# Another order for the first nine products of a fused matmul-tanh-multiply kernel, with new planned landing times, finer sums of the weights and later last multiplications

## The chip, the core and the metric

The kernel runs on one core of a Trainium2 chip. The metric is the time of one execution on the device, in microseconds (us). Before the change the median of three runs is 303.63 us, the lowest 303.56 and the highest 304.0.

The engines are named as in the profile: PE is the matrix engine (TensorE), DVE the vector engine, ACT the scalar engine, POOL the GpSimd engine, SP the engine that here only issues transfers. Each works through its own list of instructions in order. Transfers are issued by SP, ACT and POOL and then run on 16 DMA engines.

## The reference

```python
"x": np.random.randn(batch, m, k)     # 16 x 512 x 1024, float32
"w1": np.random.randn(k, n)           # 1024 x 768
"w2": np.random.randn(k, n)           # 1024 x 768

def reference(x, w1, w2):
    y1 = np.matmul(x, w1)
    y2 = np.matmul(x, w2)
    return (np.tanh(y1) * y2).astype(np.float32)
```

## The kernel before

The 8192 rows of x are 64 tiles of 128 rows. The inner dimension is 8 blocks of 128, in a lower and an upper half of 4 blocks. The columns of both weight matrices are three blocks of 512: `a` is w1[:, :512], `b` is w2[:, :512], and `g` holds the last 256 columns of w1 and of w2 side by side. Operands are cast to 16 bits, sums are float32.

**Head.** Tiles 0 to 3 are computed plainly (`plain`, `mm`, L426): per tile and column block eight matmuls, one for each inner block, while the weights arrive. One of these groups, `g` of tile 3, is left for the very end. `finals` then registers the tanh (ACT, L429) and the multiplication (DVE, L433) of a block; each frees the PSUM bank that the block occupied. There are eight banks.

**Triples.** The other 60 tiles are 20 triples of three tiles. A triple is three row tiles by two inner halves by three column blocks, which plainly would be 18 block products. The kernel does it with 15 products of sums (`C_OPS`, L24), `p0` to `p14`; each is four matmuls of 128x512 (`product`, L442). An operand is named by a mask of bits. For x, bits 1 and 2 are the lower and upper half of the triple's first tile, 4 and 8 those of the second, 16 and 32 those of the third. For w, bits 1, 2, 4 are the lower halves of blocks a, b, g and bits 8, 16, 32 their upper halves. Sums of x (`A_SUMS`; `x_sum`, L417, DVE, ten for each triple; below `S31` is the one with mask 31) are made from transposed x. Sums of w (`B_SUMS`; `w_sum`, L408, DVE, eleven in all; `B5` is the one with mask 5) are made once, in two halves of two inner blocks each.

Between the products the partial results are moved: copies and seeds on ACT (`c_copy`, L446), additions on DVE (`c_add`, L452), tanh on ACT (`c_tanh`, L455), multiplications on DVE (`c_mul`, L460). The ones that matter here: `add64` needs p7 and p10 and stands ahead of p12; `copy191` needs p12 and stands ahead of p11; `add312` needs p7 and p6 and stands ahead of p9; `seed56` needs p9 and stands ahead of both p8 and p14; `add4` comes after p3 and frees, at the end of a triple, a bank that p7 of the next but one triple takes. `abs_x` (L386, ACT) adds up the magnitudes of each x tile for a range test at the end.

**Data.** Tiles 4 to 63 of x are loaded with a cast by POOL (`load_x`, L358). From tile 7 on a transfer issued by SP transposes them (`transpose`, L383); a load waits, by a small cast on POOL (`hold_loads`, L479), until the transposition of the tile four before it has landed. Stores (L423) are on SP too, between the transpositions. The loads of `b` on POOL stand behind `gate` (L482), which waits for the first cast of `g`.

**Order.** Nothing is reordered while it runs. A planner (`Planner`, L74) puts every operation into its engine's list beforehand, with assumed costs and transfer times. The products have one fixed sequence, made of `FIRST_ORDER` (the nine products of triple 0 that start first), `PE_ORDER` (an entry with `+` runs within the following triple's fifteen) and `LAST_ORDER`. Each product has a nominal `slot_of` time, which counts from `START`. The due times of all other work are derived from these slots. A sum of x may in the plan not start before the slot of its first use less `S_AHEAD`:

```python
ORIGIN = START - 6 * SLOT
slot_of = {(i, p): ORIGIN + z * SLOT for z, i, p in sequence}
...
hold=needed(i, v) - S_AHEAD if i > 1 else 0.0,
```

When an engine is free the planner takes what can start first and, among those, what is due first (`pick`). `shared_landings` works out when the head's loads are assumed to land, from a size in us for each load and a latency for each queue. A product that begins in a new bank takes the bank that is free first; operations marked `seeds` need a bank that was last filled whole.

Every operation is one instruction, or four for a product, and each engine keeps the plan's order, so each instruction of the trace can be given its operation's name by counting along its engine. The names below are found so; `p7.10` is p7 of triple 10. Transpositions are named by tile: T36 is that of tile 36, the third tile of triple 10.

Of the kernel before, what the change touches and what calls it, by code (L numbers as in the profile page):

```python
# [66 lines left out]
)  # L67

PE_ORDER = "7 0+ 13+ 6 10 4+ 5+ 9 12 1 14 3+ 2+ 11 8"
FIRST_ORDER = "7 10 1 12 6 11 9 14 8"  # L70
LAST_ORDER = "0 13 4 5 3 2"


class Planner:  # L74
# [60 lines left out]
    def run(self):  # L135
        free = {"pe": 0.0, "act": 0.0, "dve": 0.0, "pool": 0.0, "sp": 0.0}
        bandwidth = 1.25
        left = {n: len(o["needs"] + o["behind"] + o["issued"]) for n, o in self.ops.items()}
        ready_at, end, engine_of, start_of = {n: o["hold"] for n, o in self.ops.items()}, {}, {}, {}
        ready = {e: [] for e in free}  # L140

        def release(n):
            for e in self.ops[n]["engines"]:
                ready[e].append(n)

        for n in self.ops:
            if not left[n]:
                release(n)
        position, lag = 0, 0.0
        strict = set(self.strict)  # L150
        while len(end) < len(self.ops):
            best = None
            for e, names in ready.items():
                options = []
                for n in names:
                    if n in strict and n != self.strict[position]:
                        continue
                    o = self.ops[n]
                    s = max(free[e], ready_at[n])
                    new = [c for c in o["chains"] if self.chains[c]["bank"] is None]  # L160
                    if new:
                        fit = self.fitting(o)
                        if not fit:
                            continue
                        s = max(s, min(fit)[0])
                    options.append((s, o["due"], n))
                if not options:
                    continue
                s, due, n = self.pick(e, options, lag)
                if best is None or s < best[0]:  # L170
                    best = s, e, n
            assert best, ("stuck", [(n, self.ops[n]["needs"]) for n in self.strict[position:position + 3]])
            s, e, n = best
            o = self.ops[n]
            for c in o["chains"]:
                if self.chains[c]["bank"] is None:
                    entry = min(self.fitting(o))
                    self.bank_free.remove(entry)
                    self.chains[c]["bank"] = entry[1]
                    if not o["seeds"]:  # L180
                        (self.partial.add if c[0] in ("T", "f") else self.partial.discard)(entry[1])
            f = s + o["engines"][e]
            free[e] = f
            if o["lands"]:
                done = o["lands"]
                bandwidth = max(bandwidth, done - 1.6)
            elif o["xfer"]:
                bandwidth = max(bandwidth, f) + o["xfer"]
                done = bandwidth + (o["latency"] or self.LATENCY["cast" if e == "pool" else "sp"])
            else:  # L190
                done = f
            end[n], engine_of[n], start_of[n] = done, e, s
            for k in o["engines"]:
                ready[k].remove(n)
            if n in strict:
                position += 1
                lag = s - o["due"]
            for c in o["chains"]:
                chain = self.chains[c]
                chain["end"] = max(chain["end"], done + self.LATENCY[e])  # L200
                chain["left"] -= 1
                if not chain["left"]:
                    self.bank_free.append((chain["end"], chain["bank"]))
            for u in self.next.get(n, ()):
                ready_at[u] = max(ready_at[u], f)
                left[u] -= 1
# [33 lines left out]
def kernel(  # L240
# [9 lines left out]
    B, M, K = x.shape  # L250
    _, N = w1.shape
    KO = K // P
    KH = KO // 2
# [3 lines left out]
    HEAD = 4  # L257
# [56 lines left out]
    op = plan.op  # L314
# [169 lines left out]
    MM = 0.2158  # L484
    SLOT = KH * MM
    CAST = {"a": {"dve": 0.37}, "g": {"act": 0.495}}
    START = 27.6
    ORIGIN = START - 6 * SLOT

    position = {}  # L490
# [5 lines left out]
    for n, p in enumerate(LAST_ORDER.split()):  # L496
# [7 lines left out]
    late = [f"b{k}" for s, k in slices if s == "b"]  # L504
    rows_in = (HEAD + 2, HEAD, HEAD + 1)
    GATE = ("g", 0)
    rings = [[(n, 0.75 + 0.3 * j, XW) for j, n in enumerate(on_sp)],
             [(f"a{k}", 0.75 + 0.45 * k, XW) for k in range(4)], [(n, 15.9 + 0.6 * j, 0.68) for j, n in enumerate(late)] + [(f"x{mt}", 22.0 + 0.6 * j, XX) for j, mt in enumerate(rows_in)]]
    lands = shared_landings(rings, 1.0, (2.1, 2.1, 2.6))

    for k in range(4):
# [66 lines left out]
    def finals(mt, s, due, last):  # L578
        if s != "b":
            lo, n = (0, F) if s == "a" else (F, G)  # L580
            op(f"th{s}{mt}", {"act": 0.5 if n == F else 0.28}, due, last, plain_tanh, mt, lo, n, (s, mt), 0,
               behind=reuse_out(mt), chains=[(s, mt)])
        if s != "a":
            lo, n, at = (0, F, 0) if s == "b" else (F, G, G)
            op(f"mu{s}{mt}", {"dve": 0.6 if n == F else 0.33}, due, last + [f"th{'a' if s == 'b' else s}{mt}"], plain_mul, mt, lo, n,
               (s, mt), at, chains=[(s, mt)])
            outs[mt].insert(0 if s == "b" else 1, f"mu{s}{mt}")

    for n, s in enumerate("agb"):
        for mt in range(HEAD):  # L590
            if (s, mt) == ("g", HEAD - 1):
                due, behind = (lambda n: 1e4 + n), [f"p0.{TRIPLES - 1}"]
            else:
                due, behind = (lambda n: landed[slices["agb".index(s) * KO + n]] + 0.8 + 0.02 * mt), []
            finals(mt, s, due(KO - 1) + (5.0, 3.0, 4.0)[n], plain(mt, s, due, behind))

    c_ops = {o[0]: o for o in C_OPS}
    readers = {}
# [10 lines left out]
            if u in a_readers:  # L609
                a_readers[u].append(f"S{v}")  # L610

    pieces = [slice(0, 2), slice(2, 4)]

    def w_needs(v, q):
        if v in wsum:
            return [f"B{v}.{q}"]
        bit = v.bit_length() - 1
        return [f"c{s}{k}" for s in "abg"[bit % 3] for k in range(bit // 3 * KH + pieces[q].start, bit // 3 * KH + pieces[q].stop)]

    for v, a, b, how in B_SUMS:  # L620
        for q, ks in enumerate(pieces):
            op(f"B{v}.{q}", {"dve": 0.6}, None, w_needs(a, q) + w_needs(b, q), w_sum, v, a, b, how, ks)

    def x_needs(i, v):
        if v & (v - 1):
# [13 lines left out]
    for i in range(TRIPLES):  # L639
# [10 lines left out]
        for o in C_OPS:  # L650
# [1 line left out]
            needs = [f"{n}.{i}" for n in needs]  # L652
            chains = sorted({(i, p) for p in o[3:6] if isinstance(p, str) and p[0] == "c"})
            if kind == "p":
                needs += x_needs(i, o[4]) + w_needs(o[5], 0) + w_needs(o[5], 1)
                op(f"{name}.{i}", {"pe": SLOT}, slot_of[i, name], needs, product, i, *o[3:], chains=chains)
                if not o[4] & (o[4] - 1):
                    xt_readers[HEAD + 3 * i + (o[4].bit_length() - 1) // 2].append(f"{name}.{i}")
                continue
# [35 lines left out]
    for mt in range(BY_PE, MT):  # L695
        back = xh_before(mt)
        free = [] if back is None else ([f"PT{back}0", f"PT{back}1"] if back < BY_PE else [f"T{back}"]) + ([f"D{back}"] if back >= HEAD else [])
        before = f"L{mt - 1}" if mt > BY_PE else f"L{rows_in[-1]}"
        if mt >= BY_PE + AHEAD:
            op(f"H{mt}", {"pool": 0.1}, None, [f"T{mt - AHEAD}"], hold_loads, mt - AHEAD, issued=[before])  # L700
            before = f"H{mt}"
        op(f"L{mt}", {"pool": 0.58}, None, [], load_x, mt, issued=[before], behind=free, xfer=XX)
        op(f"T{mt}", {"sp": 0.05}, None, [f"L{mt}"], transpose, mt, issued=[f"T{mt - 1}"] if mt > BY_PE else [],
           behind=xt_readers[mt - XT_BUFS] if mt >= XT_BUFS and mt - XT_BUFS != HEAD - 1 else [], xfer=1.2, latency=3.0)
    for mt in range(HEAD, MT):
        i, r = divmod(mt - HEAD, 3)
        soon = START + 1.1 * r if i == 0 else slot_of[i, "p7"] - 8 + 4.3 * r
# [125 lines left out]
```

## Time and profile before

| | us |
|---|---|
| median of three runs | 303.63 |
| profiled execution, its own time | 305.48 |
| span of the profiled execution, first to last instruction | 303.7 |
| PE busy | 291.2 |
| DVE busy | 254.0 |
| ACT busy | 224.5 |
| first product of the triples starts | 31.90 |
| last product's matmuls end | 298.12 |

The span is 1.78 us shorter than the profiled execution's own time and 0.07 us longer than the median of the runs without the profiler. A row of the timeline gives the start, the duration, the engine, the source line, what is written from what, how many instructions were merged and, in brackets, how long the engine stood idle before and what ended that. A matmul is shown with 0.38 us, but one follows the other every 0.216 us, so the idle time in the bracket is some 0.16 us less than the delay of the matmul's start. A row of the chain gives the start, the duration and what the time was spent on.

### The profile page before, as it was taken

The numbers are of one execution on the slowest core, as the hardware profiler recorded it, in microseconds if no ns is written. First come the engines' busy times: TensorE is split into PE (matmuls) and PEld (weight loads), VectorE is DVE, ScalarE is ACT, GpSimd is POOL, SyncE is SP. The second block draws the span as 40 slices with busy tenths as digits, with TensorE's granted clock in tenths as the row PEclk, the third lists the DMA queues.
The fourth block names the chain that finished last, engine by engine and source line by source line (L and its number), as shares of the span: only waits on it lengthen the run. The fifth ranks groups of instructions, "written<-read, shape, count | busy, mean of one in ns | idle before, by whom it ended". The sixth has DMA issues, their size and how long they took to land.

```text
span 303.7 us, 4640 instructions
## 1 busy us (share of the span) xinstructions
PE 291.2 (96%) x1377; PEld 133.3 (44%) x1377; DVE 254.0 (84%) x530; ACT 224.5 (74%) x451; POOL 49.6 (16%) x128
## 2 busy tenths in 40 slices
PE   8989989999999999999998999999999999999992
PEld 5435434444444444444443444444444444444440
DVE  1639999999797898978959898898989889898773
ACT  2687897688877988789787888767787767776542
POOL 0054032130301210212112111211121210000000
PEclk9999999999999999999999999999999999999999
DMA  7999999999999999999999999999999999131242
GB/s 232 385 290 208 169 124 144 175 203 236 187 158 222 190 276 281 154 205 277 210 225 241 238 245 230 249 254 190 254 280 164 299 246 253 77 155 52 104 190 92
DMA packets 84283, 63.51 MB, mean 209 GB/s; under 512 B 62752, under 2 KB 66336, under 8 KB 84256
## 3 DMA queue, kind: packets, MB, share of 16 engines
q1 hardware_dynamic: 73888, 45.36, 63.1%
q0 software_dynamic: 9792, 16.78, 38.2%
q10 hardware_dynamic: 576, 1.05, 1.0%
q8 instruction: 11, 0.18, 0.2%
q14 instruction: 16, 0.13, 0.2%
HBM read 39.85 MB, written 25.17 MB: 214 GB/s over the span
## 4 chain that ended last, share of the span: by engine, by line
PE 59%; DMA 26%; DVE 8%; ACT 2%; issue 2%; SPq 1%; ACTq 0%; POOL 0%; DVEq 0%; POOLq 0%
PE bank L442 55%; DMA xT<-xh 13%; DMA xh<-in_x_dram 7%; DMA arena<-in_w_dram 4%; PE bank L426 3%; DVE bank L452 3%; DVE o L460 2%; DVE early_x L417 2%; DMA wh<-in_w_dram 2%; ACT o L455 1%; ACT junk L386 1%; DVE arena L452 1%; PE bank L376 0%; ACTq L353 0%; DVE b L408 0%
## 5 line engine op out<-in xcount | busy, mean ns | idle before, releaser
L442 PE MATMUL bank<-b,early_x 128*128 128x512 f16 x640 | 148.4, 379 | 0.8 <-DVE arena L452 0.4
L442 PEld LDWEIGHTS <-early_x 128*128 128x128 f16 x800 | 78.1, 98 | 97.0 <-issue 3.4
L446 ACT ACTIVATE arena<-bank 128x512 f32<-128x512 f32 x100 | 58.7, 595 | 27.9 <-PE bank L442 27.8
L452 DVE TENSOR_TENSOR bank<-bank,arena 128x512 f32<-128x512 f32 x100 | 69.3, 694 | 10.5 <-ACT arena L446 4.2
L460 DVE TENSOR_TENSOR o<-o,bank 128x256 f32<-128x256 f32 (+1 forms) x120 | 63.1, 550 | 11.3 <-ACT o L455 9.9
L386 ACT ACTIVATE junk<-xh 128x1024 f16<-128x1024 f16 x60 | 63.3, 1055 | 0.3
L442 PEld LDWEIGHTS <-xT 128*128 128x128 f16 x400 | 38.9, 98 | 49.8 <-issue 4.0
L442 PE MATMUL bank<-b,xT 128*128 128x512 f16 x240 | 58.3, 379 | 0.0
L455 ACT ACTIVATE o<-bank 128x256 f32<-128x256 f32 x80 | 34.5, 437 | 18.2 <-DVE bank L452 15.8
L442 PE MATMUL bank<-wh,xT 128*128 128x512 f16 x160 | 40.9, 379 | 2.0 <-DVE bank L452 1.6
L442 PE MATMUL bank<-wh,early_x 128*128 128x512 f16 x160 | 41.0, 379 | 1.1 <-ACT bank L446 1.1
L358 POOL DMA_DIRECT2D xh<-in_x_dram x60 | 31.7, 528 | 35.4 <-PE bank L442 9.5
L479 POOL CAST held<-xT 128x1 f32<-128x1 f16 x53 | 12.8, 242 | 148.4 <-DMA xT<-xh 148.3
L417 DVE TENSOR_TENSOR early_x<-early_x,xT 128x512 f16<-128x512 f16 x80 | 31.8, 417 | 1.0 <-ACT xT L362 0.3
L446 ACT ACTIVATE bank<-bank 128x512 f32<-128x512 f32 x40 | 22.0, 579 | 11.0 <-PE bank L442 9.2
L455 ACT ACTIVATE o<-arena 128x512 f32<-128x512 f32 x40 | 25.1, 629 | 4.5 <-DVE arena L452 4.5
L426 PE MATMUL bank<-wh,xT 128*128 128x512 f16 x72 | 19.5, 379 | 1.5 <-DMA wh<-in_w_dram 0.9
L417 DVE TENSOR_TENSOR early_x<-xT,early_x 128x512 f16<-128x512 f16 x40 | 16.7, 417 | 5.0 <-DMA xT<-xh 5.0
L417 DVE TENSOR_TENSOR early_x<-xT,xT 128x512 f16<-128x512 f16 x40 | 16.7, 417 | 0.0
L452 DVE TENSOR_TENSOR bank<-arena,bank 128x512 f32<-128x512 f32 x20 | 13.8, 692 | 1.4 <-ACT o L455 1.3
L452 DVE TENSOR_TENSOR arena<-bank,arena 128x512 f32<-128x512 f32 x20 | 13.6, 679 | 0.0
L452 DVE TENSOR_TENSOR arena<-arena,bank 128x512 f32<-128x512 f32 x20 | 13.5, 677 | 0.0
(47 smaller groups left out, 133.8 us busy)
## 6 DMA issues: line engine op xcount, KB each, us to landing
out_dram<-o SPq DMA_DIRECT2D x60, 384.0 KB, 6.0
xh<-in_x_dram POOLq DMA_DIRECT2D x60, 256.0 KB, 7.1
arena<-in_w_dram SPq DMA_DIRECT2D x12, 256.0 KB, 5.5
early_x<-in_x_dram SPq DMA_DIRECT2D x8, 256.0 KB, 5.1
arena<-in_w_dram ACTq DMA_DIRECT2D x4, 256.0 KB, 5.9
wh<-in_w_dram POOLq DMA_DIRECT2D x8, 128.0 KB, 5.7
out_dram<-o SPq DMA_DIRECT2D x4, 256.0 KB, 2.5
xT<-xh SPq DMA_TRANSPOSE x57, 7.4
```

What stands on the lines that cost most here:

```text
L358: pin(nc.gpsimd.dma_start(xh(mt), xf[mt]))
L386: pin(nc.scalar.activation(junk[:, :src.shape[-1]], src, ACT.Abs, scale=scale, accum_out=sums[:, column:column + 1]))
L417: pin(engine[e].tensor_tensor(x_operand(i, v), x_operand(i, a), x_operand(i, b), OP[how]))
L426: pin(nc.tensor.matmul(bank(chain), xt(mt)[:, k, :], rhs, start=first, stop=k == KO - 1, skip_group_check=True))
L442: pin(nc.tensor.matmul(place(i, dst), x_operand(i, a)[:, k, :], w_rhs(b, k), start=begins and k == 0, stop=k == KH - 1, skip_group_check=T ...
L446: pin(nc.scalar.activation(place(i, dst), place(i, src), ACT.Copy, scale=float(sign)))
L452: pin(nc.vector.tensor_tensor(place(i, dst), a, b, ALU.add if signs == (1, 1) else ALU.subtract))
L455: pin(nc.scalar.activation(out_tile(HEAD + 3 * i + r)[:, lo:lo + n], place(i, src)[:, :n], ACT.Tanh, scale=float(sign)))
L460: pin(nc.vector.tensor_tensor(o, o, place(i, src)[:, at:at + n], ALU.mult))
L479: pin(nc.gpsimd.tensor_copy(held, xt(mt)[:, 0, :1]))
```

## The change

It has seven parts, all in what the planner is told:

1. `FIRST_ORDER` goes from `7 10 1 12 6 11 9 14 8` to `7 1 10 6 12 9 11 8 14`.
2. A product that opens a bank takes, among banks that are free in time, one that was last filled in part; before it was the one free first.
3. `START` goes from 27.6 to 28.6, and with it every slot, due time and hold of the triples.
4. The assumed sizes and start times of the head's loads are changed, which moves their assumed landings; the transposition of tiles 7, 8 and 9 gets an assumed latency of 1.0 in place of 3.0.
5. The last multiplication of a plain tile's `b` block is due 7.0 after the landing of the last weights, before 4.0.
6. The sums B5, B36, B37 and B45 (made of blocks a and g) are made in four quarters of one inner block, before in two halves.
7. A dictionary `FILL`, which is empty, changes nothing.

```diff
-FIRST_ORDER = "7 10 1 12 6 11 9 14 8"
+FIRST_ORDER = "7 1 10 6 12 9 11 8 14"
...
-                    entry = min(self.fitting(o))
+                    entry = min(self.fitting(o), key=lambda b: (b[0] > s, b[1] not in self.partial, b[0]))
...
-    START = 27.6
+    FILL = {}
+    FINE = (5, 36, 37, 45)
+    START = 28.6
...
-    rings = [[(n, 0.75 + 0.3 * j, XW) for j, n in enumerate(on_sp)],
-             [(f"a{k}", 0.75 + 0.45 * k, XW) for k in range(4)], [(n, 15.9 + 0.6 * j, 0.68) for j, n in enumerate(late)] + [(f"x{mt}", 22.0 + 0.6 * j, XX) for j, mt in enumerate(rows_in)]]
+    rings = [[(n, 0.75 + 0.3 * j, 0.75 if n[0] == "g" else 0.81 if n in ("x10", "x20", "x30") else XW) for j, n in enumerate(on_sp)],
+             [(f"a{k}", 0.75 + 0.45 * k, 0.81 if k else XW) for k in range(4)], [(n, 17.6 + 0.6 * j, 0.66) for j, n in enumerate(late)] + [(f"x{mt}", 22.0 + 0.6 * j, XX) for j, mt in enumerate(rows_in)]]
...
-            finals(mt, s, due(KO - 1) + (5.0, 3.0, 4.0)[n], plain(mt, s, due, behind))
+            finals(mt, s, due(KO - 1) + (5.0, 3.0, 7.0)["agb".index(s)], plain(mt, s, due, behind))
...
-    pieces = [slice(0, 2), slice(2, 4)]
+    PARTS = {v: 4 if v in FINE else 2 for v, *_ in B_SUMS}
+
+    def parts(v):
+        n = KH // PARTS[v]
+        return [slice(k, k + n) for k in range(0, KH, n)]
...
-        for q, ks in enumerate(pieces):
-            op(f"B{v}.{q}", {"dve": 0.6}, None, w_needs(a, q) + w_needs(b, q), w_sum, v, a, b, how, ks)
+        for ks in parts(v):
+            op(f"B{v}.{ks.start}", {"dve": {1: 0.335, 2: 0.6, 4: 1.13}[ks.stop - ks.start]}, None, w_needs(a, ks) + w_needs(b, ks), w_sum, v, a, b, how, ks)
...
-           behind=xt_readers[mt - XT_BUFS] if mt >= XT_BUFS and mt - XT_BUFS != HEAD - 1 else [], xfer=1.2, latency=3.0)
+           behind=xt_readers[mt - XT_BUFS] if mt >= XT_BUFS and mt - XT_BUFS != HEAD - 1 else [], xfer=1.2, latency=1.0 if mt < HEAD + 6 else 3.0)
```

More of the change, by code (lines that the diff above doesn't have):

```diff
@@ L593 @@
             else:
-                due, behind = (lambda n: landed[slices["agb".index(s) * KO + n]] + 0.8 + 0.02 * mt), []
-            finals(mt, s, due(KO - 1) + (5.0, 3.0, 4.0)[n], plain(mt, s, due, behind))
+                due, behind = (lambda n: landed[slices["agb".index(s) * KO + n]] + 0.8 + 0.02 * mt), [FILL[mt]] if s == "b" and mt in FILL else []
+            finals(mt, s, due(KO - 1) + (5.0, 3.0, 7.0)["agb".index(s)], plain(mt, s, due, behind))
     c_ops = {o[0]: o for o in C_OPS}
@@ L610, with w_needs @@
                 a_readers[u].append(f"S{v}")
-    pieces = [slice(0, 2), slice(2, 4)]
-    def w_needs(v, q):
+    PARTS = {v: 4 if v in FINE else 2 for v, *_ in B_SUMS}
+    def parts(v):
+        n = KH // PARTS[v]
+        return [slice(k, k + n) for k in range(0, KH, n)]
+    def w_needs(v, ks=slice(0, KH)):
         if v in wsum:
-            return [f"B{v}.{q}"]
+            return [f"B{v}.{p.start}" for p in parts(v) if p.start < ks.stop and ks.start < p.stop]
         bit = v.bit_length() - 1
-        return [f"c{s}{k}" for s in "abg"[bit % 3] for k in range(bit // 3 * KH + pieces[q].start, bit // 3 * KH + pieces[q].stop)]
+        return [f"c{s}{bit // 3 * KH + k}" for s in "abg"[bit % 3] for k in range(ks.start, ks.stop)]
     for v, a, b, how in B_SUMS:
-        for q, ks in enumerate(pieces):
-            op(f"B{v}.{q}", {"dve": 0.6}, None, w_needs(a, q) + w_needs(b, q), w_sum, v, a, b, how, ks)
+        for ks in parts(v):
+            op(f"B{v}.{ks.start}", {"dve": {1: 0.335, 2: 0.6, 4: 1.13}[ks.stop - ks.start]}, None, w_needs(a, ks) + w_needs(b, ks), w_sum, v, a, b, how, ks)
     def x_needs(i, v):
@@ L654 @@
             if kind == "p":
-                needs += x_needs(i, o[4]) + w_needs(o[5], 0) + w_needs(o[5], 1)
+                needs += x_needs(i, o[4]) + w_needs(o[5])
                 op(f"{name}.{i}", {"pe": SLOT}, slot_of[i, name], needs, product, i, *o[3:], chains=chains)
```

## The prediction

> **What bounds the kernel now.** I read the page first, then what PE waited for after 31 us, then PE's timeline, then the chain back from the largest wait, and last DVE's and ACT's timelines at those places. The page:
>
> ```profile
> span 303.7 us, 4640 instructions
> PE 291.2 (96%) x1377; PEld 133.3 (44%) x1377; DVE 254.0 (84%) x530; ACT 224.5 (74%) x451; POOL 49.6 (16%) x128
> DMA  7999999999999999999999999999999999131242
> PE 59%; DMA 26%; DVE 8%; ACT 2%; issue 2%; SPq 1%; ACTq 0%; POOL 0%; DVEq 0%; POOLq 0%
> ```
>
> PE is the bound by its length, but a quarter of the chain is transfers, and the DMA engines are busy in all slices to about 255 us. What PE waited for after 31 us:
>
> ```profile
> PE bank L442 <- DVE bank L452: 2.0, 3, 1.2
> PE bank L442 <- ACT bank L446: 1.1, 1, 1.1
> PE bank L442 <- DVE arena L452: 0.4, 1, 0.4
> PE bank L442 <- DVE o L460: 0.4, 1, 0.4
> ```
>
> These 3.9 us are all that a new order behind 31.9 us can win. PE's timeline shows where they lie:
>
> ```profile
> 22.36 0.81 PE L426 MATMUL bank<-wh,xT 128*128 128x512 f16 x3 [0.95 <-DMA wh<-in_w_dram]
> 31.90 1.89 PE L442 MATMUL bank<-wh,xT 128*128 128x512 f16 x8
> 33.63 1.03 PE L442 MATMUL bank<-b,early_x 128*128 128x512 f16 x4
> 35.06 3.83 PE L442 MATMUL bank<-b,early_x 128*128 128x512 f16 x16 [0.41 <-DVE arena L452]
> 39.99 1.02 PE L442 MATMUL bank<-wh,early_x 128*128 128x512 f16 x4 [1.09 <-ACT bank L446]
> 41.71 1.03 PE L442 MATMUL bank<-wh,xT 128*128 128x512 f16 x4
> 42.58 1.03 PE L442 MATMUL bank<-b,xT 128*128 128x512 f16 x4
> 55.29 1.02 PE L442 MATMUL bank<-wh,xT 128*128 128x512 f16 x4 [0.40 <-DVE o L460]
> 81.81 1.02 PE L442 MATMUL bank<-wh,xT 128*128 128x512 f16 x4 [0.46 <-DVE bank L452]
> 160.82 1.02 PE L442 MATMUL bank<-wh,xT 128*128 128x512 f16 x4 [1.16 <-DVE bank L452]
> 292.87 1.89 PE L442 MATMUL bank<-b,early_x 128*128 128x512 f16 x8 [0.34 <-DVE bank L452]
> ```
>
> An undisturbed product takes 0.865 us (from 41.71, p7.1, to 42.58, the next). The nine products of triple 0 run from 31.90 to 41.71: 9.81 us against 9 x 0.865 = 7.79, so 2.0 us are lost there. p12 starts at 35.06 where 33.63 + 0.865 = 34.50 would do: 0.57. Its group of 16 matmuls (p12, p6, p11, p9) and p14 behind it hold the other 1.45. The rows at 55.29, 81.81 and 160.82 are p7.2, p7.4 and p7.10; with 0.16 us added to each bracket they lose 0.56, 0.62 and 1.32. Without any of these waits p7.10 would start at 160.82 - 2.0 - 0.56 - 0.62 - 1.32 = 156.3.
>
> The chain back from the waits at 81.81 and 160.82, and what follows:
>
> ```profile
> 70.33 9.54 DMA xT<-xh
> 131.01 9.53 DMA xT<-xh
> 141.18 6.74 DMA xh<-in_x_dram
> 147.97 10.92 DMA xT<-xh
> 160.82 123.62 PE bank L442 x572
> ```
>
> The transposition T36 was issued at 147.97 and landed at 147.97 + 10.92 = 158.89; T18 at 79.87. Behind T36 stands the load of tile 36 (141.18), and behind that the landing of T32 (131.01 + 9.53 = 140.54): a loop of transfers that contains no product. From T32's landing to T36's are 18.35 us for four tiles, while PE needs 4/3 of 15 x 0.865 = 17.3. So in this stretch transfers set the pace. After 160.82 PE runs 123.6 us without a wait: a gain that stands at p7.10 reaches the end, and one that doesn't is lost.
>
> **The change part by part.** DVE's, ACT's and POOL's rows that carry the terms:
>
> ```profile
> 18.33 1.29 DVE L408 TENSOR_TENSOR b<-wh 128x1024 f16<-128x1024 f16 x2 [3.27 <-ACT wh L362]
> 22.84 1.29 DVE L408 TENSOR_TENSOR b<-wh 128x1024 f16<-128x1024 f16 x2 [1.76 <-ACT wh L362]
> 33.73 0.68 DVE L433 TENSOR_TENSOR o<-o,bank 128x512 f32<-128x512 f32 x1
> 34.33 0.68 DVE L452 TENSOR_TENSOR arena<-arena,bank 128x512 f32<-128x512 f32 x1
> 37.73 0.41 DVE L417 TENSOR_TENSOR early_x<-early_x 128x512 f16<-128x512 f16 x1
> 38.06 0.41 DVE L417 TENSOR_TENSOR early_x<-xT 128x512 f16<-128x512 f16 x1
> 51.62 0.41 DVE L417 TENSOR_TENSOR early_x<-xT 128x512 f16<-128x512 f16 x1
> 158.98 0.42 DVE L417 TENSOR_TENSOR early_x<-xT,early_x 128x512 f16<-128x512 f16 x1 [2.24 <-DMA xT<-xh]
> 159.32 0.74 DVE L460 TENSOR_TENSOR o<-o,bank 128x256 f32<-128x256 f32 x2
> 159.99 0.69 DVE L452 TENSOR_TENSOR bank<-arena,bank 128x512 f32<-128x512 f32 x1
> 22.17 1.16 ACT L362 CAST wh<-arena 128x512 f16<-128x512 f32 x2
> 38.30 1.06 ACT L386 ACTIVATE junk<-xh 128x1024 f16<-128x1024 f16 x1
> 39.27 0.19 ACT L386 ACTIVATION_READ_ACCUMULATOR junk<-xh 128x1 f32 x1
> 39.36 0.58 ACT L446 ACTIVATE bank<-bank 128x512 f32<-128x512 f32 x1
> 50.99 0.41 POOL L479 CAST held<-xT 128x1 f32<-128x1 f16 x1 [9.86 <-DMA xT<-xh]
> ```
>
> *Planned landings (part 4): nothing before 31.90.* No transfer is issued elsewhere. The wait at 22.36 is for the first `b` weights, and what could run ahead of it, the last `g` products, needs the casts that end only at 22.17 + 1.16 = 23.33. From 22.36 PE works through 38 plain matmuls and three tiles of transposes without a gap, in whatever order. Ends: -0.95 (that wait gone) to +0.87 (one group of four matmuls put ahead of its load). I take 0.
>
> *Order of the nine (part 1): -1.2 us of PE, between -2.0 and 0.* Every dependent pair now has one whole product between: p10, p6, p12 for `add64`; p6, p12, p9 for `add312`; p12, p9, p11 for `copy191`; p9, p11, p8 for `seed56`, where before p14 stood right behind p9. That gap is 0.865 - 0.16 = 0.70 us. An addition takes 0.69, so it fits with 0 to 0.1 left over; a seed takes 0.58. What can spoil it is ACT: at 38.30 a magnitude sum of 1.06 + 0.19 kept `seed56` waiting until 39.36, and such a sum may again stand ahead of it. At worst 1.25 of it is in the way, against a slack of 0.1; I take 0.75, for a sum begun a little earlier. The lower end of nothing is two such sums.
>
> *Late multiplications (part 5): included above.* The one at 33.73 is what delayed `add64` to 34.33, so p12 to 35.06. Moved back, it and its three fellows hold four banks for longer. Part 2 hands the first products the partly filled banks; p7's bank is free for `add312`. The first that needs one of the four is `seed56`; if its multiplication came late, that would cost one, 0.68. These 2.7 us of DVE work then stand among the sums for p0 and p13. The cover there is the quarters' gain, next.
>
> *Quarters (part 6): 0 on the path.* DVE idles 3.27 + 1.76 = 5.0 us around 18 to 23, waiting for casts of `g`. Four sums in quarters take 16 instructions every 0.33 us (37.73 to 38.06, the same shape) or 5.3, against eight at some 0.6 (two in 1.29, the ends overlapping), 4.8: 0.5 more, inside that idle time. Since a quarter waits for one cast pair, all four sums are done soon after 23.3; before, two of their halves ran later, in DVE's busy stretch. That takes 1.2 us out of it, less 0 to 0.5. The Trainium skill (Perfetto Trace Analysis, Optimizing Scalar/DVE Operations) says that each DVE operation on SBUF carries about 60 ns of its own, so larger ones are better on a saturated engine, but that breaking up can help where DVE isn't saturated and holds others up. By its figure eight more instructions are an estimated 0.5 us, and the trace agrees with that; DVE is idle there, so the second half of the rule applies.
>
> *START and the holds (part 3): decides where the gain ends.* On DVE S31.10 (158.98) waited 2.24 us for T36, and behind it in line stood two multiplications and `add4.8` (159.99), ready long before, for whose bank p7.10 waited. S31's hold is its slot less 4. Slots move 1.0 later. The planned start of the products also moves later, by about the 1.6 us that the first `b` load's assumed landing moves (1.7 for its start, little for the sizes), but the planned waits among the nine go, which as the trace has them are 2.0. So the holds fall about 1 us (0.2 to 1.4) behind the same products, and `add4`, 1.0 us behind S31 here, is likely to go first. Then only T36 itself holds p7.10: 158.89 + 0.05 = 158.94, where it was 160.82: -1.88. The same holds at p7.4: T18 at 79.87 for 81.81.
>
> *Transposition latency, slots against transfers: +0.3 on DVE, covered.* T10 landed just before 50.99 and S3.2 ran at 51.62. With PE and DVE 1.2 us earlier S3.2 waits for it, some 0.5 us, with everything behind it: p7.2, 3.7 us after S3.2 here, comes no earlier than 50.95 + 3.67 = 54.6 (-0.7). From there eight triples of 12.97 give 158.4, still below 158.94.
>
> The sum: 303.70 - 1.88 = 301.8 for the span; it stands 0.07 above the median, so 301.75 for the runs. The early gains of 0.7 to 4.5 us are worth 1.88 because T36 cuts them off, and 0.5 us of new early waits change nothing.
>
> **The rivals.** A change within 0.2% (0.6 us) is about what a measurement of this kernel can't tell from none.
>
> 1. *S31.10 stays ahead of `add4.8`.* Then DVE waits for T36 as before, and p7.10 starts at 160.8: 303.6. Against it: a hold moved by 0.1 us is enough if the multiplications behind are ready. Chance 0.14.
> 2. *Transfers come earlier too.* The loop is started by tile 10's load, which waits for a magnitude sum on ACT; transposition and store places on SP shift as well. p7.10 can go to 156.3 + 0.75 = 157.0, which is 299.8; half of it, 300.8. Against it: T36's chain has no product in it. Chance 0.2.
> 3. *Slower: one more store, or a late sum on ACT, puts the transfer loop back.* The loop's place is 36 to 159 us, its price 18.35/4 = 4.6 us for a tile's turn. Once T36 lands after 161.4 (2.5 us later, half a turn) the kernel is slower by over 0.6; a whole turn gives 158.94 + 4.6, 2.7 us over before: 306.3. For it: DMA busy at 9 tenths throughout, and stores that are ready earlier compete with the same transfers. The Trainium skill (DMA: Bandwidth & Descriptors, Issuing engines are not separate DMA queues) says that transfers from all issuing engines run on the same 16 DMA engines and interleave; the slices agree, and by that rule a faster PE wins no transfer time. Chance 0.18.
>
> **How the numbers follow.** My forecast, p7.10 held by T36 alone, has 0.48; T36 varies with neighbours by some 0.7 us, so its own range is 301.1 to 302.5. Faster: 0.48 + 0.2 = 0.68; same 0.14; slower 0.18. The range runs from 300.2, where a third of rival 2 is left out, to 304.4, where most of rival 3 is.
>
> **What would show it.** PE's timeline: p7.0 still at 31.9; the nine take 8.2 to 8.8 us; no wait over 0.8 among them. DVE: quarters of the sums between 17 and 24.5, no 128x1024 sum of `a` and `g` behind. p7.10 at 158.9 with its bracket naming the transfer, not DVE, and S31.10 behind `add4.8`. After that no wait to 284. Wrong would be: T36 away from 158.9 by over 1.5 us, p7.10 still waiting for DVE, or a new wait after 160 us.

## The result, and the profile after

Six runs of the changed kernel have a median of 301.83 us (301.65 to 302.66), six of the kernel before 303.7 (303.46 to 304.0). The ratio is 0.9943, with a 95% interval of 0.9931 to 0.9956: some 1.9 us less by the medians. A ratio compares only runs within 1.5% of the fastest run of their kernel; a median is over all runs. The forecast was 301.75. The number came out; the mechanism did not, as follows.

The page of the kernel after:

```profile
span 300.4 us, 4674 instructions
PE 290.8 (97%) x1377; PEld 132.8 (44%) x1377; DVE 255.8 (85%) x538; ACT 224.9 (75%) x451; POOL 52.5 (17%) x128
DMA  6999999999999999999999999999999999231243
PE 84%; DMA 7%; DVE 5%; issue 1%; ACT 1%; ACTq 0%; SPq 0%; POOL 0%; DVEq 0%
```

The profiled execution took 302.25 us by its own time. Transfers are 7% of the chain, where they were 26%. What PE waited for after 31 us is down from 3.9 us to 1.2:

```profile
PE bank L442 <- DVE o L460: 0.5, 1, 0.5
PE bank L442 <- DVE arena L452: 0.4, 1, 0.4
PE bank L442 <- DVE bank L452: 0.3, 1, 0.3
```

PE's timeline of after, at the places the prediction named:

```profile
32.09 1.03 PE L442 MATMUL bank<-wh,xT 128*128 128x512 f16 x4
36.09 3.70 PE L442 MATMUL bank<-b,early_x 128*128 128x512 f16 x16 [0.39 <-DVE arena L452]
40.75 1.04 PE L442 MATMUL bank<-wh,xT 128*128 128x512 f16 x4
54.42 1.02 PE L442 MATMUL bank<-wh,xT 128*128 128x512 f16 x4 [0.50 <-DVE o L460]
80.31 1.03 PE L442 MATMUL bank<-wh,xT 128*128 128x512 f16 x4
158.01 1.03 PE L442 MATMUL bank<-wh,xT 128*128 128x512 f16 x4
281.00 0.17 PE L473 MATMUL bank<-count,ones 128*128 128x8 bf16 x1
290.38 1.89 PE L442 MATMUL bank<-b,early_x 128*128 128x512 f16 x8 [0.34 <-DVE bank L452]
```

The nine products run from 32.09 to 40.75, 8.66 us (before: 9.81). p7.4 (80.31) and p7.10 (158.01) have no bracket: the two waits on which the forecast stood are gone, but the hold by T36, which the forecast put in their place, is not there either. The next rows are from POOL's timeline of after. They are the small casts that wait for T10 and for T36:

```profile
42.81 0.18 POOL L479 CAST held<-xT 128x1 f32<-128x1 f16 x1 [1.01 <-DMA xT<-xh]
144.05 0.20 POOL L479 CAST held<-xT 128x1 f32<-128x1 f16 x1
```

T10 had landed by 42.8 (before: 50.9). The cast behind T36 runs at 144.05 and did not wait for it; by the transfer's own record T36 landed at 141.85, 17 us earlier than the 158.89 that the forecast took for fixed.

The last DVE instructions and the last four stores of after, from the timeline of its end:

```profile
295.08 2.59 SPq L423 DMA_DIRECT2D out_dram<-o  x4
295.82 1.34 DVE L460 TENSOR_TENSOR o<-o,bank 128x256 f32<-128x256 f32 x3
```

The last multiplication ends at 295.82 + 1.34 = 297.16, and 3.2 us later the span is over. In the kernel before the same row stood as follows, and from its end at 299.65 to 303.7 it took 4.05 us:

```profile
298.31 1.34 DVE L460 TENSOR_TENSOR o<-o,bank 128x256 f32<-128x256 f32 x3
```

So the gain has a term at the very end that the prediction did not have.

### The profile page after: what moved, and what is told of

The parts are those of the page before. It is cut to its first block, busy times and chain, and to the rows that moved or that the text cites. A ratio compares the mean times of both kernels' runs of the same rounds, so it can differ in the third digit from the quotient of the medians.

```text
span 300.4 us, 4674 instructions
## 1 busy us (share of the span) xinstructions
PE 290.8 (97%) x1377; PEld 132.8 (44%) x1377; DVE 255.8 (85%) x538; ACT 224.9 (75%) x451; POOL 52.5 (17%) x128
## 3 DMA queue, kind: packets, MB, share of 16 engines
q10 hardware_dynamic: 576, 1.05, 1.0%
## 4 chain that ended last, share of the span: by engine, by line
PE 84%; DMA 7%; DVE 5%; issue 1%; ACT 1%; ACTq 0%; SPq 0%; POOL 0%; DVEq 0%
PE bank L442 80%; DMA arena<-in_w_dram 4%; PE bank L426 3%; DMA wh<-in_w_dram 2%; DMA xT<-xh 1%; DVE bank L452 1%; DVE o L460 1%; DVE early_x L417 1%; DVE arena L452 1%; ACT o L455 1%; PE bank L376 0%; ACTq L353 0%; DVE b L408 0%; ACT wh L362 0%; SPq L350 0%
## 5 line engine op out<-in xcount | busy, mean ns | idle before, releaser
L452 DVE TENSOR_TENSOR bank<-bank,arena 128x512 f32<-128x512 f32 x100 | 69.5, 695 | 19.1 <-ACT arena L446 13.2
L460 DVE TENSOR_TENSOR o<-o,bank 128x512 f32<-128x512 f32 (+1 forms) x120 | 61.1, 549 | 4.9 <-ACT o L455 3.2
L455 ACT ACTIVATE o<-bank 128x256 f32<-128x256 f32 x80 | 33.0, 436 | 12.4 <-DVE bank L452 8.2
L479 POOL CAST held<-xT 128x1 f32<-128x1 f16 x53 | 15.6, 295 | 39.5 <-DMA xT<-xh 39.4
```

The source lines that it names most:

```text
L452: pin(nc.vector.tensor_tensor(place(i, dst), a, b, ALU.add if signs == (1, 1) else ALU.subtract))
L455: pin(nc.scalar.activation(out_tile(HEAD + 3 * i + r)[:, lo:lo + n], place(i, src)[:, :n], ACT.Tanh, scale=float(sign)))
L460: pin(nc.vector.tensor_tensor(o, o, place(i, src)[:, at:at + n], ALU.mult))
L479: pin(nc.gpsimd.tensor_copy(held, xt(mt)[:, 0, :1]))
```

## The experiments

After the comparison three theories stood. The first is the forecast's: in the kernel before, T36 and what stands behind it on DVE hold p7.10 in every execution, and the new plan takes away DVE's part of that. The second: the new landings let the planner put the magnitude sum of tile 4 early, tile 10's load with it, and all transfers run ahead from there. The third: the profiled execution of before was not a typical one, and the gain comes from other places. All kernels compute the whole result.

**The kernel before once more** (no edit).

> The kernel before once more, for a second profiled execution. The first one took 305.48 us, 1.85 above the median of the plain runs, and lost 0.62 + 1.32 us at p7.4 and p7.10 to late transpositions. Theory A (the prediction's: T36 lands at 158.9 and caps everything): p7.10 again starts at 160 to 161, T36 lands at 158 to 159.5. Theory C (those two waits belong to that one execution): T36 lands at 157 or earlier, p7.10 loses under 0.3 us, the span is 301.5 to 302.5. Time 303.6 under either.

Measured: 303.94 us, ratio 0.998 (0.9946 to 1.0014); span of its profile 302.2. PE's timeline, POOL's cast behind T36, and ACT's magnitude sum of tile 4:

```profile
31.86 1.89 PE L442 MATMUL bank<-wh,xT 128*128 128x512 f16 x8
41.67 1.03 PE L442 MATMUL bank<-wh,xT 128*128 128x512 f16 x4
55.24 1.02 PE L442 MATMUL bank<-wh,xT 128*128 128x512 f16 x4 [0.40 <-DVE o L460]
81.24 1.02 PE L442 MATMUL bank<-wh,xT 128*128 128x512 f16 x4
158.94 1.02 PE L442 MATMUL bank<-wh,xT 128*128 128x512 f16 x4
```
```profile
148.58 0.18 POOL L479 CAST held<-xT 128x1 f32<-128x1 f16 x1 [2.88 <-DMA xT<-xh]
```
```profile
34.69 1.06 ACT L386 ACTIVATE junk<-xh 128x1024 f16<-128x1024 f16 x1
```

The same program, and T36 lands at 148.5 in place of 158.9; p7.4 and p7.10 wait for nothing. The waits among the nine and at p7.2 are the same as in the first profile. The forecast's theory falls: the two waits, 0.62 + 1.32 = 1.94 us, come in some executions and not in others. That execution took 305.48 us, 1.85 above the median of the plain runs; this one took 303.98, close to its median. Two more profiled executions further down, of kernels close to before, have one such wait each (0.69 at p7.4 in 305.39 us, 1.37 at p7.10 in 305.26 us). So this profile is the one to compare with:

| stretch | before, second profile | after | difference |
|---|---|---|---|
| start to p7.0 | 31.86 | 32.09 | +0.23 |
| p7.0 to p7.1, nine products | 9.81 | 8.66 | -1.15 |
| p7.1 to p7.2 | 13.57 | 13.67 | +0.10 |
| p7.2 to the last multiplication's end | 242.53 | 242.74 | +0.21 |
| from there to the span's end | 4.4 | 3.2 | -1.2 |
| span | 302.2 | 300.4 | -1.8 |

The +0.21 is the matmul of the range test: by the starts of the products around it, it costs 0.32 us in after (at 281.00) and 0.11 here. A third of the gain (0.6) lies ahead of the last multiplication's end, two thirds behind it. The rows of this execution's end:

```profile
295.69 3.61 SPq L423 DMA_DIRECT2D out_dram<-o  x4
296.43 1.34 DVE L460 TENSOR_TENSOR o<-o,bank 128x256 f32<-128x256 f32 x3
```

The four stores take 3.61 us to issue, against 2.59 in after; by its own record the last of them takes 1.40 us here and 0.38 there. The view of the DMA queues for the last 6.2 us of this kernel shows what else ran there (queue, kind, packets, MB, share; then the stores with KB each and us to landing):

```profile
q14 instruction: 3, 0.02, 1.8%
q8 instruction: 1, 0.02, 1.6%
...
out_dram<-o SPq DMA_DIRECT2D x3, 128.0 KB, 3.2
```

And for the last 4.9 us of after:

```profile
q14 instruction: 1, 0.01, 0.5%
...
out_dram<-o SPq DMA_DIRECT2D x2, 128.0 KB, 1.8
```

Transfers that fetch instructions run among the last stores. In the kernel before, one of queue 8 and three of queue 14 fall there, and a store lands after 3.2 us; in after one of queue 14, and a store lands after 1.8. Two runs further down test this.

**The new order alone, in the kernel before.**

```diff
-FIRST_ORDER = "7 10 1 12 6 11 9 14 8"
+FIRST_ORDER = "7 1 10 6 12 9 11 8 14"
```

> Before with the new order of the first nine products alone. Theory A: the nine take about 8.7 us in place of 9.8, but T36 stays at 158.9 and S31.10 stays ahead of add4.8, so the time stays at 303.4 to 303.7. Theory B (the gain needs the transfers to run ahead, which the magnitude sum of tile 4 decides, and its place does not change here): the same, 303.4 to 303.7, with T10 landing near 50. Theory C (the medians gained only what the nine products gained): 302.4 to 302.8.

Measured: 304.09 us, ratio 1.0006 (0.9977 to 1.0036). DVE, then PE:

```profile
33.79 1.88 DVE L433 TENSOR_TENSOR o<-o,bank 128x512 f32<-128x512 f32 x3
...
36.26 0.68 DVE L452 TENSOR_TENSOR arena<-arena,bank 128x512 f32<-128x512 f32 x1
```
```profile
36.99 3.88 PE L442 MATMUL bank<-b,early_x 128*128 128x512 f16 x16 [1.42 <-DVE arena L452]
```

Three multiplications of plain tiles stand ahead of `add64` (36.26), and p12 loses 1.58 us. The nine take 9.62 us, and the order by itself is worth nothing. T10 landed at 43.63 here, not near 50 as the expectation had it, and T36 at 144.94, though the magnitude sum of tile 4 had not moved; the transfers ran ahead and the time did not fall.

**The change without the later due time.**

```diff
-            finals(mt, s, due(KO - 1) + (5.0, 3.0, 7.0)["agb".index(s)], ...
+            finals(mt, s, due(KO - 1) + (5.0, 3.0, 4.0)["agb".index(s)], ...
```

> The changed kernel with the plain tiles' last multiplications due 4.0 after the weights, as before. With the new order alone, put into before, add64 stood behind three such multiplications and p12 lost 1.58 us. Theory: here too they go ahead of add64, p12 loses 1.2 to 1.8, the nine take 9.5 to 10 us and the time is 302.6 to 303.4. If the late due time is idle: 301.8.

Measured: 303.62 us, ratio 0.9969 (0.9946 to 0.9991). DVE, then PE:

```profile
34.98 1.88 DVE L433 TENSOR_TENSOR o<-o,bank 128x512 f32<-128x512 f32 x3
36.77 0.68 DVE L452 TENSOR_TENSOR arena<-arena,bank 128x512 f32<-128x512 f32 x1
```
```profile
37.50 3.78 PE L442 MATMUL bank<-b,early_x 128*128 128x512 f16 x16 [1.82 <-DVE arena L452]
```

The same picture from the other side: p12 loses 1.98 us and the nine take 9.91. Without the late multiplications the order does not pay. p7.2 starts 0.51 later than in after (54.93), and the end takes 4.38 us.

**The magnitude sum of tile 4 put back, in the changed kernel.**

```diff
-        op(f"D{mt}", ..., mt, hold=soon)
+        op(f"D{mt}", ..., mt, hold=soon + (4.0 if mt == HEAD else 0.0))
```

> The changed kernel with one thing more: the magnitude sum of tile 4 (D4) may not start before 4.0 us later in the plan, so on ACT it goes back behind the copy of p7, as before the change. In the changed kernel it ran at 30.2 us and the load of tile 10 was issued at 31.6 in place of 36.2. Theory B (D4's place puts all transfers ahead): T10 lands near 50 again, T36 near 158, the time is 302.8 to 303.5. Theory C: the transfers may come later but the time stays within 0.5 of the changed kernel's, 301.8 to 302.3. Theory A: T36 at 158.9 and a time of 301.7 to 302, as it had been forecast.

Measured: 303.79 us, ratio 0.9986 (0.9957 to 1.0016). POOL's cast behind T10, and PE at p7.2:

```profile
51.18 0.37 POOL L479 CAST held<-xT 128x1 f32<-128x1 f16 x1 [8.89 <-DMA xT<-xh]
```
```profile
55.09 1.02 PE L442 MATMUL bank<-wh,xT 128*128 128x512 f16 x4 [0.96 <-DVE o L460]
```

T10 lands at 51.06 again, x sums stand behind it on DVE, and p7.2 loses 0.67 of its gain. T36 lands at 154.98, p7.4 and others wait too, and no gain can be told from this ratio. So it matters that the new plan starts this sum at 30.18 and not at 34.7:

```profile
30.18 1.07 ACT L386 ACTIVATE junk<-xh 128x1024 f16<-128x1024 f16 x1
```

**That sum put early, in the kernel before.**

```diff
-        op(f"D{mt}", {"act": 1.05}, soon + 4, ...
+        op(f"D{mt}", {"act": 1.05}, -10.0 if mt == HEAD else soon + 4, ...
```

> Before with one thing changed: the magnitude sum of tile 4 is due first, so it goes ahead of the evacuations of tiles 4 and 5 on ACT, some 5 us earlier. Nothing else is told to the planner. Theory B: the load of tile 10 is issued by 32, T10 lands by 45, T36 by 145, the waits at p7.4 and p7.10 go and the time falls by 1 to 2 us, to 301.7 to 302.7; the nine products still take 9.8 us or some tenths more. Theory C: the transfers go ahead but the time stays at 303.4 to 304. Theory A: T36 moves little, 303.6.

Measured: 305.07 us, from 302.99 to 321.53 with five of twelve runs above 309, ratio 0.9986 (0.9964 to 1.0007). POOL's casts behind T10 and T36:

```profile
42.07 1.06 POOL L479 CAST held<-xT 128x1 f32<-128x1 f16 x1
...
158.48 0.44 POOL L479 CAST held<-xT 128x1 f32<-128x1 f16 x1 [4.29 <-DMA xT<-xh]
```

T10 lands early, at 41.76, and T36 late all the same, at 158.36, and p7.10 loses 1.37 us to it. The nine take 9.11 us, 0.7 less than in before, yet p7.2 starts at 55.33, no earlier. The second theory falls as a sufficient cause: an early start of the loop doesn't keep the transfers ahead. The early sum is needed in the new plan and brings nothing in the old one.

**More matmuls ahead of everything, in the kernel before.** The warm-up, which writes nothing that is used, gets 40 short matmuls in place of 14 long ones.

```diff
-    WARM = 14
+    WARM = 40
...
-    pin(nc.tensor.matmul(banks[...][:, :2 * P], ..., ones.bitcast(bf16), ...
+    pin(nc.tensor.matmul(banks[...][:, :88], ..., ones.bitcast(bf16)[:, :88], ...
```

> Before with 26 matmuls more in PE's list and as many columns as before in all: the 14 warming matmuls of 256 columns at the start become 40 of 88 columns (they compute nothing that is used). So PE's instructions stand 52 places later in its list. In three profiles of before's end an instruction fetch of 16 KB on queue 8 began 0.3 to 0.4 us before the last multiplication ended, and the end followed 4.1 to 4.45 us after that multiplication; in the changed kernel the fetch came 5.9 us before it, and the end 3.2 after. Theory D (the fetch slows the last stores, and its place follows the count of PE's instructions): the fetch moves some 5.5 us ahead, the end follows 3.1 to 3.4 us after the last multiplication, and the time falls by 0.8 to 1.2 us, to 302.5 to 302.9. Rival (the end differs for another reason): 4.1 to 4.5 us, time 303.5 to 304.

Measured: 304.07 us, ratio 0.9994 (0.997 to 1.0018). The fetch of queue 8 moved from 0.3 us to 13.2 us ahead of the last multiplication's end, further than the 5.5 expected. In the second profile of before, 218 to 305 PE instructions lie between one fetch of this queue and the next, so the queue very likely serves PE. In this profile the longer warm-up also put p7.0 at 32.73, 0.87 us later. But the end still took 4.37 us, and the view of its DMA queues has three fetches of queue 14 left there:

```profile
q14 instruction: 3, 0.02, 1.5%
...
out_dram<-o SPq DMA_DIRECT2D x2, 128.0 KB, 2.4
```

PE's fetch alone is not it.

**Idle instructions on three engines, in the kernel before.**

```diff
-    WARM = 14
+    WARM = 20
...
+    for n in range(20):
+        pin(nc.vector.memset(idle[:, :1], 0.0))
...
+    for n in range(8):
+        pin(nc.scalar.copy(idle[:, 1:2], ones[:, :1]))
```

> Before with small idle instructions added at the start, where each engine stands idle: 20 one-column fills on DVE, 8 one-column copies on ACT, and the warming matmuls as 20 of 176 columns in place of 14 of 256. The planned order stays. Moving PE's fetch alone did not shorten the end, since fetches on queue 14 remained 0.5 and 1.3 to 1.9 us after the last multiplication. Theory D, extended (any engine's instruction fetch among the last stores costs time, and its place follows the count of that engine's instructions): the fetches on queues 8 and 14 leave the stretch from 0.4 before to 1.9 us after the last multiplication, the end follows 3.1 to 3.5 us after it, before 4.05 to 4.45, and the time falls by 0.7 to 1.2. Rival: the end stays at 4.0 to 4.5 whatever the fetches do; 303.6 to 304.2.

Measured: 303.22 us, ratio 0.9974 (0.995 to 0.9998); beside it the kernel before had 304.15. PE's times stay as before (p7.1 at 41.59, p7.2 at 55.17). The end, and its DMA queues:

```profile
295.52 2.59 SPq L424 DMA_DIRECT2D out_dram<-o  x4
...
296.26 1.34 DVE L461 TENSOR_TENSOR o<-o,bank 128x256 f32<-128x256 f32 x3
```
```profile
q14 instruction: 1, 0.01, 0.6%
...
out_dram<-o SPq DMA_DIRECT2D x2, 128.0 KB, 1.8
```

From 297.60 to the span's end at 300.8 are 3.2 us, as in after. The last multiplication ends 0.17 us earlier than in the second profile of before, so all but that of the shorter span is the end. Work that does nothing makes the old kernel 0.9 us faster by the medians (0.1 to 1.5 by the interval), and in the profile the fetches have left the last stores. That is the term of -1.2 us, shown by itself.

**The change without quarters.**

```diff
-    FINE = (5, 36, 37, 45)
+    FINE = ()
```

> The changed kernel with the four w sums in halves again. Theory: the first quarter runs beside POOL's gate cast, which took 0.43 us in place of 0.18, so the b loads started 0.2 later; in halves the gate takes 0.18, the first b weights land near 22.3 and p7.0 starts at 31.85 in place of 32.09. Against that two halves return to DVE's busy stretch behind 24 us and p7.2 comes 0.3 to 1.2 later than that gains. Time 301.9 to 302.7. If the quarters do nothing: 301.6, by the gate alone.

Measured: 302.86 us, ratio 0.9953 (0.9926 to 0.9981). The nine take 8.04 us, less than with quarters, but p7.2 starts at 54.44, as in after. POOL's gate ahead of the `b` loads takes 0.18 us here and 0.44 in after, where it runs beside DVE's quarters; `b` still lands at 22.46 and p7.0 starts at 32.05. So the long gate is not why p7.0 is 0.2 late in after. The end takes 4.39 us, with queue 8's fetch in it. The quarters alone do not decide that: the change without the later due time has them, and its end takes 4.38 us with the same fetch. In this profile the quarters pay nothing ahead of p7.2; whether the better end is theirs is not shown.

**The change with the old order.**

```diff
-FIRST_ORDER = "7 1 10 6 12 9 11 8 14"
+FIRST_ORDER = "7 10 1 12 6 11 9 14 8"
```

> The changed kernel with the old order of the first nine products. Theory (the prediction's first term): p14 behind p9 waits for its seed again, the nine take 9.5 to 10 us in place of 8.66, p7.2 starts 0.7 to 1.3 later than 54.42, and the time is 302.5 to 303.2. Rival: what the nine give is taken by DVE's backlog before p7.2 in any case; then p7.2 stays within 0.3 of 54.4, and the time at 301.8 to 302.

Measured: 303.27 us, ratio 0.9974 (0.9956 to 0.9993). PE's timeline:

```profile
54.19 1.02 PE L442 MATMUL bank<-wh,xT 128*128 128x512 f16 x4
```

The nine take 9.06 us, 0.4 more, and p7.2 starts at 54.19, no later than in after. What the order wins among the nine, DVE's backlog ahead of p7.2 takes back; in these profiles the other parts do the early gain without it. From p7.0 to p7.2 the profiles have, in us:

| kernel | p7.0 to p7.2 |
|---|---|
| before, both profiles | 23.39, 23.38 |
| before with the new order | 23.52 |
| before with the early sum | 23.48 |
| after | 22.33 |
| after with the old order | 22.34 |
| after without quarters | 22.39 |
| after without the later due time | 22.86 |
| after with the late sum | 23.02 |

So of the gain of 1.05 us there, the later due time holds 0.53, the early sum 0.69 and the order nothing; the two overlap. The end takes 3.86 us with the old order. Since the profile puts this kernel within 0.3 us of after's span and the medians are 1.4 apart in different comparisons, how much the order is worth in typical runs stays open.

**Three attempts at a faster kernel.** The first lets the gate run ahead of DVE's quarters and sends the range test's matmul to the end:

```diff
+               issued=["B36.0"] if (v, ks.start) == (5, 0) else [])
...
-    op("f4", {"pe": 0.1}, ORIGIN, ...
+    op("f4", {"pe": 0.1}, ORIGIN + 15 * SLOT * TRIPLES, ...
```

> The changed kernel with two small edits: the first quarter of B5 stands behind that of B36, so no DVE sum runs while the gate's cast does; and the flag's small matmul is due at the end, so PE does not wait for its count ahead of p12.19. Theory: the gate takes 0.18, p7.0 starts at 31.85 to 31.9, PE loses nothing at the flag (0.29 before), and the time falls by 0.4 to 0.5, to 301.3 to 301.4. If the gate is not it: p7.0 at 32.05 to 32.1, time 301.5 to 301.6.

Measured: 302.22 us, ratio 0.9931 (0.9907 to 0.9956). PE's timeline:

```profile
40.76 1.04 PE L442 MATMUL bank<-wh,xT 128*128 128x512 f16 x4 [0.47 <-DMA xT<-xh]
```

The wait at p12 shrinks to 0.19, but p7.1 starts where it did in after, 0.05 behind the landing of T9 in both (40.71 here, 40.70 in after). p7.0 stays at 32.09, though the gate takes 0.19. The flag's matmul no longer costs PE 0.32 at 281, but the last multiplication now ends 3.89 us after the last two products begin, where it was 3.43. The second adds tile 9's load and transposition ahead of those of 7 and 8:

```diff
-    for mt in range(BY_PE, MT):
+    first = [BY_PE + 2, BY_PE, BY_PE + 1]
+    for mt in first + list(range(BY_PE + 3, MT)):
```

> The changed kernel with the gate and flag edits and the loads and transpositions of triple 1 in the order tile 9, 7, 8, since p7.1 waited for tile 9 (0.63 us in the kernel with those two edits alone). Theory: T9 lands at 38 to 39, p7.1 starts at 39.9 to 40.2. If DVE's backlog is the next bound, p7.2 stays at 54.2 to 54.6 and the time at 301.6; if not, p7.2 starts at 53.5 to 53.9, and the time falls by 0.6.

Measured: 302.11 us, ratio 0.9936 (0.9917 to 0.9956). PE's timeline:

```profile
54.10 1.02 PE L442 MATMUL bank<-wh,xT 128*128 128x512 f16 x4 [0.79 <-DVE o L460]
```

T9 lands at 36.91 and p7.1 starts at 40.13, 0.62 earlier than in after; 0.31 of that is p7.0, which starts at 31.78. p7.2 keeps 0.32 in all, and waits for DVE: what T9 gave is lost there. The third takes the sum B48 from DVE to POOL:

```diff
+ {"pool": 2.2} if v == 48 else {"dve": ...}
```

> The same with B48 made by POOL between 25 and 31 us, where POOL is idle, in place of DVE near 50: 1.2 us off DVE's backlog ahead of p7.2. Theory: p7.2 starts 0.5 to 0.8 earlier than without, 53.4 to 53.9, and the time is 301.0 to 301.3. Rival: POOL's sums slow DVE's, which run beside them and read the same memory, by as much as they save: p7.2 within 0.3 of the kernel without.

Measured: 307.59 us, ratio 1.0112 (1.0085 to 1.0138). DVE, then POOL:

```profile
25.66 5.71 DVE L408 TENSOR_TENSOR b<-wh 128x1024 f16<-128x1024 f16 x2
```
```profile
26.59 4.23 POOL L408 TENSOR_TENSOR b<-wh 128x1024 f16<-128x1024 f16 x2
```

Two sums that take 1.28 us on DVE elsewhere take 5.71 here: the second of them (26.26 to 31.37) ends only after both of POOL's. p1 then waits 4.3 us. The Trainium skill (SBUF — State Buffer, SBUF: two separate sides) says that DVE and GpSimd share one pair of ports, which an operation holds whole while the other is blocked, also for a DVE operation with two inputs from SBUF. The trace agrees that DVE waited, and DVE didn't get in between POOL's two. By the records DVE's sum began 0.33 us ahead of POOL's first, though; which of them held the ports first is not settled by this trace. Neither of the first two attempts can be told from after, and the third is slower.

## Why the prediction was right and wrong

**START and the holds, T36 as the end of the gain (-1.88): wrong, and this is the step that failed.** I took two waits of one execution for waits of the kernel. The sign was on the page: the profiled execution took 305.48 us and the median was 303.63. I set the *span* of 303.70 against that median and wrote that it stood 0.07 above, where the execution's own time stood 1.85 above, nearly the 1.94 of the two waits. Against a typical execution the term is 0. I also let T36 vary by 0.7 us; two executions of one program put it 10.4 us apart, and after has it at 141.85, 16 us before p7.10 starts. `S31.10` behind `add4.8`, the rival's point, decided nothing. What happened is the rival in which transfers come earlier: it had the place of the sum on ACT right, and the span of 300.4 lies in its 299.8 to 300.8, but that time counted the same two waits as won and did not have the end.

**Order of the nine (-1.2): right for the length of the nine, wrong as a cause.** Measured 1.15, within the stated -2.0 to 0. With the old order put back the nine lose 0.40 of it and p7.2 loses nothing, so the rest comes from the other parts. Of what is left, 0.55 is p12's, because `add64` starts late on DVE, and 0.26 is p7.1's behind T9's landing; neither is a magnitude sum on ACT.

**Late multiplications ("included above"): right, and stronger than said.** Without them the order gives nothing, by the two runs that separate them; with them 0.75 of the 1.15 comes without the order (9.06 against 9.81).

**Transposition latency, T10 holding S3.2 (p7.2 at 54.6): right number, wrong wait.** p7.2 started at 54.42, but T10 had landed at 42.69. The plan moved tile 4's magnitude sum from 34.7 to 30.2, which I had not seen; the wait at p7.2 is DVE's own backlog, `o L460` in the bracket.

**Quarters (0 on the path): right for the front,** where p7.2 is the same without them. What more instructions do to the fetches at the end I had left out.

**p7.0 at 31.9: 32.09,** since `b` lands at 22.50 in place of 22.27 to 22.32, within the bounds of -0.95 to +0.87.

**No wait from p7.10 to 284: nearly;** only the range test's 0.32 at 281.

**Missing altogether: the end, -1.2.** Without the end, the terms as measured give 303.63 + 0.2 - 1.15 + 0.1 + 0.2, some 303.0. The forecast let T36 cut off the front's 0.6 and did not have the end's 1.2; together they are 1.8, nearly the 1.88 that it counted for the two waits. So 301.75 was met by luck. The spans show it: 301.8 was forecast and 300.4 measured, a fall of 3.3 us from the profile that the forecast was worked out from, where it said 1.9.

Open: why `b` lands 0.2 later (with the old order put back it landed at 22.27 again), why the transfers run ahead in one execution and behind in another, which engine each fetch of queue 14 serves, and which part of the change moved the fetches.

## What to carry to other kernels

Before a wait is priced, hold the profiled execution's own time, not its span, against the median of the plain runs: what it is longer by lay here in two transfer waits that the next execution didn't have. When two kernels differ by a per cent or less, compare the time from the last instruction that computes to the end as a stretch of its own, and look for instruction fetches in it. Idle instructions moved them here, and so did a mere change of ACT's order: with the early sum in the kernel before, queue 8's fetch went from 0.3 to 5.9 us ahead of the last multiplication's end.

## What the runs showed of the hardware

Fetches of instructions run among the last stores and delay them. Queue 8 has 11 packets of 16 KB in each run, queue 14 fetches 8 KB at a time. The table is read from the records of the transfers; its times count from the end of the last multiplication, in us, and fetches of queue 14 are given within 4 us of it. The fourth column is when the last of the 16 parts of the last store landed:

| kernel | fetch of queue 8 | fetches of queue 14 | last part of the last store | end takes |
|---|---|---|---|---|
| before, second profile | -0.38 | 0.55, 1.3, 3.12 | 3.28 | 4.43 |
| before with 40 warming matmuls | -13.2 | 0.53, 1.88, 2.1 | 3.23 | 4.37 |
| before with idle instructions | -7.2 | -3.02, 2.12 | 2.08 | 3.23 |
| after | -5.85 | 2.11 | 2.07 | 3.22 |
| after without quarters | -0.36 | 0.7, 1.3, 3.08 | 3.24 | 4.39 |
| after without the later due time | -0.38 | -3.67, 3.06 | 3.24 | 4.38 |
| after with the old order | -5.92 | -3.65, 0.53, 2.11 | 2.72 | 3.86 |

Over all fourteen profiles, the five with no fetch that begins between 0.4 us before and 2 us after the last multiplication's end have ends of 3.2 to 3.4 us, and the nine with one have 3.9 to 4.5. In all fourteen the span ends 1.14 to 1.22 us after the last part of a store has landed. So the end waits for the stores. With the old order put back, 15 of the last store's 16 parts land by 2.09, near the 2.07 of after, and one at 2.72; that fits a fetch, which takes 0.57 us there, on one of the DMA engines that carry the parts. Where a fetch of queue 8 runs there, the last store also takes 0.9 to 1.4 us to issue in place of 0.38. An engine that only waited for its own instructions would not explain late parts of a store. The kernel ends with a branch around the path for inputs that fail the range test; whether the fetches of queue 14 belong to it is not known.

The Trainium skill (Runtime: NRT & Kernel Launch, Instruction fetch mechanics) says that instructions come in 16 KiB blocks over a queue of their own, and that crossing a block is "mostly hidden". The size agrees for queue 8; at the end of this kernel the fetches were not hidden, at a price of 0.6 to 1.2 us by the profiles and some 0.9 by the runs with idle instructions.

The same transposition of the same program landed 10 us apart in two executions (T36 at 158.89 and 148.46), and only the later one held PE up.
